# A batched fp32 matmul computed in bf16: manual order, four-byte pair transposes, chunked last loads, and two stores moved behind the last load

## The chip, the cores and the metric

One core of a Trainium2 chip. Times are device microseconds (us), medians of fast runs. Besides its times each kernel has one profiled execution; its *span*, from the first to the last instruction, is 1.7 to 1.9 us shorter than the time of that same execution. In the profiles PE is TensorE, PEld its weight loads, DVE VectorE, ACT ScalarE, POOL GpSimd, SPq the queue that issues the stores.

## The reference

`x` is (32, 512, 1024) fp32, `weight` is (32, 1024, 768) fp32, the output is (32, 512, 768) fp32:

```python
def reference(x, weight):
    return np.matmul(x, weight).astype(np.float32)
```

Each of the 32 batches reads 2.10 MB of x and 3.15 MB of weight and writes 1.57 MB: 218.1 MB altogether. The kernels load with a cast to bf16.

## The kernel before

One batch after another; the Tile scheduler orders the instructions. `x` has its rows on the partitions, so each 128 x 128 block is transposed on TensorE with an identity, copied from PSUM to SBUF, and used as the stationary operand.

```python
w_pool = ...bufs=3; x_pool = ...bufs=3; xT_pool = ...bufs=4; out_pool = ...bufs=3
tpsum = ...bufs=4 (PSUM); mpsum = ...bufs=4 (PSUM)
for b in range(B):
    wb_sb = w_pool.tile([P, KT, N], BF16)
    nc.gpsimd.dma_start(out=wb_sb, in_=w_view[b])
    x_sb = x_pool.tile([P, MT, K], BF16)
    nc.gpsimd.dma_start(out=x_sb, in_=x_view[b])
    out_sb = out_pool.tile([P, MT, N], F32)
    for mt in range(MT):                       # 4 row tiles
        xT_sb = xT_pool.tile([P, KT, P], BF16)
        for j in range(KT):                    # 8 transposes and 8 copies
            pt = tpsum.tile([P, P], BF16)
            nc.tensor.transpose(pt, x_sb[:, mt, j::KT], ident)
            nc.any.tensor_copy(xT_sb[:, j, :], pt)
        for (noff, nsz) in N_SPLITS:           # 512 and 256 columns
            pm = mpsum.tile([P, nsz], F32)
            ...8 matmuls...
            nc.any.tensor_copy(out_sb[:, mt, noff:noff + nsz], pm)
    nc.sync.dma_start(out_view[b], out_sb)
```

Of the kernel before, what the change touches and what calls it, by code (L numbers as in the profile page):

```python
# [1 line left out]

# [5 lines left out]

F32 = mybir.dt.float32
BF16 = mybir.dt.bfloat16  # L10


@with_exitstack
def kernel(
    ctx: ExitStack,
    tc: tile.TileContext,
    x: bass.AP,
    weight: bass.AP,
    out: bass.AP,
):  # L20
    nc = tc.nc
    B, M, K = x.shape
    _, _, N = weight.shape
    P = 128
    assert M % P == 0 and K % P == 0
    MT = M // P
    KT = K // P

    N_SPLITS = []
    off = 0  # L30
    while off < N:
        sz = min(512, N - off)
        N_SPLITS.append((off, sz))
        off += sz

    const = ctx.enter_context(tc.tile_pool(name="const", bufs=1))
    ident = const.tile([P, P], BF16)
    make_identity(nc, ident)

    w_pool = ctx.enter_context(tc.tile_pool(name="w", bufs=3))  # L40
    x_pool = ctx.enter_context(tc.tile_pool(name="x", bufs=3))
    xT_pool = ctx.enter_context(tc.tile_pool(name="xT", bufs=4))
    out_pool = ctx.enter_context(tc.tile_pool(name="out", bufs=3))
    tpsum = ctx.enter_context(tc.tile_pool(name="tpsum", bufs=4, space=bass.MemoryType.PSUM))
    mpsum = ctx.enter_context(tc.tile_pool(name="mpsum", bufs=4, space=bass.MemoryType.PSUM))

    w_view = weight.rearrange("b (ki ko) n -> b ki ko n", ki=P)
    x_view = x.rearrange("b (mi mo) k -> b mi mo k", mi=P)
    out_view = out.rearrange("b (mi mo) n -> b mi mo n", mi=P)

    for b in range(B):
        wb_sb = w_pool.tile([P, KT, N], BF16)
        nc.gpsimd.dma_start(out=wb_sb, in_=w_view[b])  # L53

        x_sb = x_pool.tile([P, MT, K], BF16)
        nc.gpsimd.dma_start(out=x_sb, in_=x_view[b])  # L56

        out_sb = out_pool.tile([P, MT, N], F32)

        for mt in range(MT):  # L60
            xT_sb = xT_pool.tile([P, KT, P], BF16)
            for j in range(KT):
                pt = tpsum.tile([P, P], BF16)
                nc.tensor.transpose(  # L64
                    pt,
                    x_sb[:, mt, j::KT],
                    ident,
                )
                nc.any.tensor_copy(xT_sb[:, j, :], pt)  # L69

            for (noff, nsz) in N_SPLITS:
                pm = mpsum.tile([P, nsz], F32)
                for j in range(KT):
                    nc.tensor.matmul(  # L74
                        pm,
                        xT_sb[:, j, :],
                        wb_sb[:, j, noff:noff + nsz],
                        start=(j == 0),
                        stop=(j == KT - 1),
                    )  # L80
                nc.any.tensor_copy(out_sb[:, mt, noff:noff + nsz], pm)  # L81

        nc.sync.dma_start(out_view[b], out_sb)


# [1 line left out]
_INS = ['x', 'weight']  # L87
_OUTS = [((32, 512, 768), 'float32')]


# [23 lines left out]
```

## Time and profile before

531.46 us (530.21 to 531.87 in three runs), span 528.3 us.

| | before |
|---|---|
| TensorE (PE) busy | 435.0 us, 82% |
| DMA packets, share of 16 engines' span | loads 75.6%, stores 23.0% |
| TensorE idle for weights | 43.8 us |
| first matmul that the last load released, TensorE ends, span ends | 508.7, 521.9, 528.3 us |

The first lines are from the page of the kernel before: DMA busy in tenths over 40 slices, the two big queues, and the two groups of TensorE (busy us, mean ns; then idle time before them and its releaser).

```profile
DMA  8999999999999999999999999999999999999962
q0 software_dynamic: 9216, 83.89, 75.6%
q1 hardware_dynamic: 4608, 50.33, 23.0%
...
L74 PE MATMUL pm<-wb_sb,xT_sb 128*128 128x512 bf16 (+1 forms) x1991 | 382.5, 334 | 47.0 <-DMA wb_sb<-in_weight_dram 43.8
...
L64 PE MATMUL pt<-ident,x_sb 128*128 128x128 bf16 x1024 | 126.7, 226 | 40.0 <-DVE xT_sb L69 22.4
```

DMA is full in every slice but the first and the last two. TensorE is busy 82% and still waits for weights; the other engines idle more. The bound is the transfers. Windows show where they are not full. Columns: start and end, length, busy us of PE, PE weight loads, DVE, ACT and POOL with instruction counts, granted TensorE clock (as a share of full speed), DMA share, and GB/s as written (a load counts with its bf16 bytes, half of what it reads).

```profile
50.00:450.00 400.00, 341.17 (x2376) 225.97 (x2420) 81.38 (x404) 175.09 (x606) 26.37 (x50) 0.97 1.02 265
...
505.00:510.00 5.00, 2.74 (x22) 1.97 (x22) 0.81 (x4) 1.73 (x6) 0.00 (x0) 1.00 0.80 256
510.00:515.00 5.00, 4.82 (x38) 3.34 (x37) 0.81 (x4) 2.31 (x7) 0.00 (x0) 1.00 0.28 118
515.00:520.00 5.00, 4.59 (x36) 3.12 (x36) 1.61 (x8) 2.87 (x11) 0.00 (x0) 1.00 0.01 3
520.00:525.00 5.00, 1.93 (x13) 1.08 (x11) 0.00 (x0) 0.96 (x2) 0.00 (x0) 1.00 0.38 157
```

From 50 to 450 us the DMA share is 1.02 (packets overlap a little, so it can pass 1). After 512 us DMA is nearly idle while TensorE computes the last batch, whose weights have just landed. The timeline shows both ends of that stretch (start us, length, engine, line, instruction; in brackets the idle time before and its releaser):

```profile
508.70 0.38 PE L74 MATMUL pm<-wb_sb,xT_sb 128*128 128x512 bf16 x1 [2.03 <-DMA wb_sb<-in_weight_dram]
...
519.38 2.55 PE L74 MATMUL pm<-wb_sb,xT_sb 128*128 128x512 bf16 x15
...
522.37 0.33 SPq L83 DMA_DIRECT2D out_dram<-out_sb  x1
```

### The profile page before, as it was taken

The numbers are of one execution on the slowest core, as the hardware profiler recorded it, in microseconds if no ns is written. First come the engines' busy times: TensorE is split into PE (matmuls) and PEld (weight loads), VectorE is DVE, ScalarE is ACT, GpSimd is POOL, SyncE is SP. The second block draws the span as 40 slices with busy tenths as digits, with TensorE's granted clock in tenths as the row PEclk, the third lists the DMA queues.
The fourth block names the chain that finished last, engine by engine and source line by source line (L and its number), as shares of the span: only waits on it lengthen the run. The fifth ranks groups of instructions, "written<-read, shape, count | busy, mean of one in ns | idle before, by whom it ended". The sixth has DMA issues, their size and how long they took to land.

```text
span 528.3 us, 7878 instructions
## 1 busy us (share of the span) xinstructions
PE 435.0 (82%) x3015; PEld 287.6 (54%) x3072; DVE 103.4 (20%) x515; ACT 222.8 (42%) x766; POOL 34.6 (7%) x70
## 2 busy tenths in 40 slices
PE   0799979977988897799879889987988897888984
PEld 0466656654656565466545555654555565565653
DVE  0122211211212121122212122221222121221211
ACT  0145534443444344344434444443444344443442
POOL 3000000000000000000000000000000000000000
PEclk9999999998999899899989998998999899998998
DMA  8999999999999999999999999999999999999962
GB/s 163 213 217 276 278 266 268 275 272 257 244 267 273 275 258 269 252 260 275 276 263 244 261 268 273 260 277 257 246 273 275 271 248 265 255 274 275 252 209 120
DMA packets 13861, 134.72 MB, mean 255 GB/s; under 512 B 1536, under 2 KB 1536, under 8 KB 1536
## 3 DMA queue, kind: packets, MB, share of 16 engines
q0 software_dynamic: 9216, 83.89, 75.6%
q1 hardware_dynamic: 4608, 50.33, 23.0%
q8 instruction: 24, 0.39, 0.3%
q14 instruction: 13, 0.11, 0.0%
HBM read 167.77 MB, written 50.33 MB: 413 GB/s over the span
## 4 chain that ended last, share of the span: by engine, by line
issue 81%; DMA 9%; POOL 6%; PE 2%; POOLq 0%; DVE 0%; ACT 0%
DMA wb_sb<-in_weight_dram 6%; POOL wb_sb L53 3%; POOL x_sb L56 3%; DMA x_sb<-in_x_dram 3%; PE pm L74 2%; PE pt L64 0%; DVE xT_sb L69 0%; POOLq L53 0%; POOLq L56 0%; ACT out_sb L81 0%; POOL ident masks.py:199 0%; POOL ident masks.py:197 0%; POOLq masks.py:199 0%; POOLq L109 0%; POOLq L98 0%
## 5 line engine op out<-in xcount | busy, mean ns | idle before, releaser
L74 PE MATMUL pm<-wb_sb,xT_sb 128*128 128x512 bf16 (+1 forms) x1991 | 382.5, 334 | 47.0 <-DMA wb_sb<-in_weight_dram 43.8
L74 PEld LDWEIGHTS <-xT_sb 128*128 128x128 bf16 x2048 | 200.2, 100 | 158.3 <-issue 49.7
L81 ACT COPY out_sb<-pm 128x512 f32<-128x512 f32 (+1 forms) x256 | 122.7, 479 | 207.1 <-PE pm L74 192.6
L69 DVE COPY xT_sb<-pt 128x128 bf16<-128x128 bf16 x515 | 103.4, 222 | 416.3 <-PE pt L64 400.8
L64 PE MATMUL pt<-ident,x_sb 128*128 128x128 bf16 x1024 | 126.7, 226 | 40.0 <-DVE xT_sb L69 22.4
L69 ACT COPY xT_sb<-pt 128x128 bf16<-128x128 bf16 x509 | 111.9, 273 | 91.8 <-PE pt L64 91.3
L64 PEld LDWEIGHTS <-x_sb 128*128 128x128 bf16 x1024 | 102.2, 148 | 75.7 <-issue 48.8
L56 POOL DMA_DIRECT2D x_sb<-in_x_dram x32 | 17.0, 530 | 385.7 <-PE pt L64 385.7
L53 POOL DMA_DIRECT2D wb_sb<-in_weight_dram x32 | 17.1, 533 | 54.2 <-PE pt L64 53.8
L69 ACT ACT_TABLE_LOAD x1 | 1.3, 1283 | 0.7 <-PEq L98 0.7
masks.py:199 POOL TENSOR_SCALAR_AFFINE_SELECT ident<-ident 128x128 bf16<-128x128 bf16 x1 | 0.3, 305 | 0.1
masks.py:197 POOL MEMSET ident<- 128x128 bf16 x1 | 0.2, 205 | 0.3 <-POOLq L98 0.3
L98 POOL MEMSET const-float32-0.0<- 128x1 f32 x1 | 0.1, 98 | 0.2 <-issue 0.2
L98 POOL MEMSET const-bfloat16-1.0<- 128x1 bf16 x1 | 0.1, 101 | 0.0
L98 POOL MEMSET const-uint8-127<- 128x1 uint8 x1 | 0.1, 101 | 0.0
L98 POOL MEMSET const-float32-1.0<- 128x1 f32 x1 | 0.1, 98 | 0.0
## 6 DMA issues: line engine op xcount, KB each, us to landing
wb_sb<-in_weight_dram POOLq DMA_DIRECT2D x32, 1536.0 KB, 34.0
out_dram<-out_sb SPq DMA_DIRECT2D x32, 1536.0 KB, 14.6
x_sb<-in_x_dram POOLq DMA_DIRECT2D x32, 1024.0 KB, 27.0
```

Of the source, the lines that this page charges most:

```text
L53: nc.gpsimd.dma_start(out=wb_sb, in_=w_view[b])
L56: nc.gpsimd.dma_start(out=x_sb, in_=x_view[b])
L64: nc.tensor.transpose(pt, x_sb[:, mt, j::KT], ident,)
L69: nc.any.tensor_copy(xT_sb[:, j, :], pt)
L74: nc.tensor.matmul(pm, xT_sb[:, j, :], wb_sb[:, j, noff:noff + nsz], start=(j == 0), stop=(j == KT - 1),)
L81: nc.any.tensor_copy(out_sb[:, mt, noff:noff + nsz], pm)
L98: nc = _bacc.Bacc("TRN2", target_bir_lowering=False, num_devices=1)
```

## The change

Its intent is to shorten the head and tail and to take work off the engines. x is viewed as fp32 pairs of bf16, so 16 four-byte transposes replace 32 per batch; four share one PSUM bank and one DVE copy. Two row tiles share a tile of three banks, evicted by ACT (1024 columns) and DVE (512). The order is written by hand and loads run four batches ahead. The last two weights come in chunks of (4, 4) and (3, 3, 1, 1) of the 8 rows that a partition holds, with all 16 transposes of such a batch first. The stores of batches 29 and 30 are queued on the load queue behind the last load. Cut to its core:

```diff
+    CHUNKED = {B - 2: (4, 4), B - 1: (3, 3, 1, 1)}
+    HELD = {B - 3, B - 2}
...  # w and x pools 3 -> 5, xT 4 -> 6, out 3 -> 5; tpsum and mpsum 4 -> 2 each
+    def load_w(b):
+        ...
+        for n in CHUNKED.get(b, (KT,)):
+            nc.gpsimd.dma_start(out=ws[b][:, at:at + n, :], in_=w_view[b, :, at:at + n, :])
+    def transpose(b, mt):
+        pt = tpsum.tile([P, JT, P], F32, name="pt")
+        pairs = xs[b].bitcast(F32)
+        for j in range(JT):
+            nc.tensor.transpose(pt[:, j, :], pairs[:, mt, j::JT], ident)
+        xT = xT_pool.tile([P, JT, P, 2], BF16, name="xT")
+        nc.vector.tensor_copy(...)             # 1024 bf16 columns at once
+    def evacuate(b, pair, pm):
+        o = outs[b]
+        nc.scalar.copy(o[:, pair * N2:pair * N2 + 1024], pm[:, 0:1024])
+        nc.vector.tensor_copy(o[:, pair * N2 + 1024:(pair + 1) * N2], pm[:, 1024:N2])
+    with tc.manual_schedule():
+        ...  # x before w; loads of batch b + 4 are issued at batch b
+        for b in range(B):
+            outs[b] = out_pool.tile([P, MT * N], F32, name="out_sb")
+            if b not in CHUNKED:
+                xT = {mt: transpose(b, mt) for mt in (0, 1)}
+                ...  # a pair of row tiles at a time; transposes of tiles 2, 3 in between
+                if b in HELD:
+                    continue
+                nc.sync.dma_start(out_view[b], outs[b])
+            else:
+                xT = {mt: transpose(b, mt) for mt in range(MT)}
+                ...  # chunk by chunk over all four row tiles; the last batch stores by pairs
+            if b == B - 2:
+                for h in sorted(HELD):
+                    nc.gpsimd.dma_start(out=out_view[h], in_=outs[h])
```

More of the change, by code (lines that the diff above doesn't have):

```diff
@@ L24 @@
     P = 128
-    assert M % P == 0 and K % P == 0
     MT = M // P
     KT = K // P
-    N_SPLITS = []
-    off = 0
-    while off < N:
-        sz = min(512, N - off)
-        N_SPLITS.append((off, sz))
-        off += sz
-    const = ctx.enter_context(tc.tile_pool(name="const", bufs=1))
-    ident = const.tile([P, P], BF16)
-    make_identity(nc, ident)
-    w_pool = ctx.enter_context(tc.tile_pool(name="w", bufs=3))
-    x_pool = ctx.enter_context(tc.tile_pool(name="x", bufs=3))
-    xT_pool = ctx.enter_context(tc.tile_pool(name="xT", bufs=4))
@@ L43 @@
-    out_pool = ctx.enter_context(tc.tile_pool(name="out", bufs=3))
-    tpsum = ctx.enter_context(tc.tile_pool(name="tpsum", bufs=4, space=bass.MemoryType.PSUM))
-    mpsum = ctx.enter_context(tc.tile_pool(name="mpsum", bufs=4, space=bass.MemoryType.PSUM))
+    JT = KT // 2
+    N2 = 2 * N
+    CHUNKED = {B - 2: (4, 4), B - 1: (3, 3, 1, 1)}
+    HELD = {B - 3, B - 2}
+    const = ctx.enter_context(tc.tile_pool(name="const", bufs=1))
+    w_pool = ctx.enter_context(tc.tile_pool(name="w", bufs=5))
@@ L47 @@
+    x_pool = ctx.enter_context(tc.tile_pool(name="x", bufs=5))
+    xT_pool = ctx.enter_context(tc.tile_pool(name="xT", bufs=6))
+    out_pool = ctx.enter_context(tc.tile_pool(name="out", bufs=5))
+    tpsum = ctx.enter_context(tc.tile_pool(name="tpsum", bufs=2, space=bass.MemoryType.PSUM))
+    mpsum = ctx.enter_context(tc.tile_pool(name="mpsum", bufs=2, space=bass.MemoryType.PSUM))
     w_view = weight.rearrange("b (ki ko) n -> b ki ko n", ki=P)
     x_view = x.rearrange("b (mi mo) k -> b mi mo k", mi=P)
-    out_view = out.rearrange("b (mi mo) n -> b mi mo n", mi=P)
@@ L51 @@
-    for b in range(B):
-        wb_sb = w_pool.tile([P, KT, N], BF16)
-        nc.gpsimd.dma_start(out=wb_sb, in_=w_view[b])
-        x_sb = x_pool.tile([P, MT, K], BF16)
-        nc.gpsimd.dma_start(out=x_sb, in_=x_view[b])
-        out_sb = out_pool.tile([P, MT, N], F32)
-        for mt in range(MT):
-            xT_sb = xT_pool.tile([P, KT, P], BF16)
-            for j in range(KT):
-                pt = tpsum.tile([P, P], BF16)
-                nc.tensor.transpose(
-                    pt,
-                    x_sb[:, mt, j::KT],
-                    ident,
-                )
-                nc.any.tensor_copy(xT_sb[:, j, :], pt)
-            for (noff, nsz) in N_SPLITS:
-                pm = mpsum.tile([P, nsz], F32)
-                for j in range(KT):
-                    nc.tensor.matmul(
-                        pm,
-                        xT_sb[:, j, :],
-                        wb_sb[:, j, noff:noff + nsz],
-                        start=(j == 0),
-                        stop=(j == KT - 1),
-                    )
-                nc.any.tensor_copy(out_sb[:, mt, noff:noff + nsz], pm)
-        nc.sync.dma_start(out_view[b], out_sb)
+    out_view = out.rearrange("b (mi mo) n -> b mi (mo n)", mi=P)
@@ new lines, with load_x @@
+    xs, ws, outs = {}, {}, {}
+    def load_x(b):
+        xs[b] = x_pool.tile([P, MT, K], BF16, name="x_sb")
+        nc.gpsimd.dma_start(out=xs[b], in_=x_view[b])
+    def load_w(b):
+        ws[b] = w_pool.tile([P, KT, N], BF16, name="w_sb")
+        at = 0
+        for n in CHUNKED.get(b, (KT,)):
+            nc.gpsimd.dma_start(out=ws[b][:, at:at + n, :], in_=w_view[b, :, at:at + n, :])
+            at += n
+    def transpose(b, mt):
[4 more added lines that the diff above has]
+        xT = xT_pool.tile([P, JT, P, 2], BF16, name="xT")
+        nc.vector.tensor_copy(
+            xT.rearrange("p j m r -> p (j m r)"), pt.bitcast(BF16).rearrange("p j m -> p (j m)")
+        )
+        return xT
@@ new lines, with matmuls @@
+    SPLITS = (((0, 512), (512, N - 512)), ((0, 1024 - N), (1024 - N, N2 - 1024)))
+    def matmuls(pm, half, xT, b, kos, together):
+        for ko in kos:
+            for i, (off, size) in enumerate(SPLITS[half]):
+                shares = half == 1 and i == 0
+                nc.tensor.matmul(
+                    pm[:, half * N + off:half * N + off + size],
+                    xT[:, ko // 2, :, ko % 2],
+                    ws[b][:, ko, off:off + size],
+                    start=(ko == 0 and not (together and shares)),
+                    stop=(ko == KT - 1),
+                    skip_group_check=together,
+                )
@@ new lines, in evacuate @@
+    def evacuate(b, pair, pm):
[3 more added lines that the diff above has]
+    with tc.manual_schedule():
+        load_x(0)
+        load_w(0)
+        ident = const.tile([P, P], F32)
+        make_identity(nc, ident)
+        for b in range(1, 4):
+            load_x(b)
+            load_w(b)
+        for b in range(B):
+            if b + 4 < B:
+                load_x(b + 4)
+                load_w(b + 4)
+            outs[b] = out_pool.tile([P, MT * N], F32, name="out_sb")
+            if b not in CHUNKED:
+                xT = {mt: transpose(b, mt) for mt in (0, 1)}
+                for pair in range(2):
+                    pm = mpsum.tile([P, N2], F32, name="pm")
+                    for half in range(2):
+                        if pair == 0:
+                            matmuls(pm, half, xT[half], b, range(KT), False)
+                            xT[2 + half] = transpose(b, 2 + half)
+                        else:
+                            matmuls(pm, half, xT[2 + half], b, range(KT), False)
+                    evacuate(b, pair, pm)
+                if b in HELD:
+                    continue
+                nc.sync.dma_start(out_view[b], outs[b])
+            else:
+                xT = {mt: transpose(b, mt) for mt in range(MT)}
+                pms = [mpsum.tile([P, N2], F32, name="pm") for _ in range(2)]
+                at = 0
+                for n in CHUNKED[b]:
+                    for mt in range(MT):
+                        matmuls(pms[mt // 2], mt % 2, xT[mt], b, range(at, at + n), True)
+                        if at + n == KT and mt % 2 == 1:
+                            evacuate(b, mt // 2, pms[mt // 2])
+                            if b not in HELD:
+                                pair = mt // 2
+                                nc.sync.dma_start(
+                                    out_view[b, :, pair * N2:(pair + 1) * N2],
+                                    outs[b][:, pair * N2:(pair + 1) * N2],
+                                )
+                    at += n
+            if b == B - 2:
+                for h in sorted(HELD):
+                    nc.gpsimd.dma_start(out=out_view[h], in_=outs[h])
```

## The prediction

> **What bounds it now.** The DMA engines, not TensorE. The page's slices show DMA at 90% or more in 38 of 40 slices; its queue table gives loads 75.6% and stores 23.0% of 16 engines' span. PE is 82% busy and waits 43.8 us for weights. In the chain of waits, x loads are issued from 31.5 to 472.2 us in 28 steps, 15.74 us a batch; a batch moves 5.24 MB in (fp32) and 1.57 MB out, so about 430 GB/s. The Trainium skill ("DMA: Bandwidth & Descriptors", section "Where 436 GB/s comes from") gives a ceiling of 435; the trace agrees. All 218.1 MB at 428 to 433 GB/s is 504 to 510 us, starting about 3 us in. The kernel's only sizeable waste is the tail: windows of 5 us show DMA share 0.28, 0.01, 0.38, 0.37 after 510. The last load lands at 508.7, PE works 13.3 us on the last batch (timeline), the last store takes from 522.4 to 528.3. The measured time is 3.1 us above the span.
>
> **What the change does not touch.** Bytes, the fp32-to-bf16 cast in the load, descriptor sizes (8 and 12 KB). Prefetch of five instead of three batches feeds a queue that is never empty. So 15.7 to 15.9 us a batch stays.
>
> **What it removes and adds on the engines.** 1024 bf16 transposes become 512 four-byte ones. Their cost is my main unknown: no trace shows one. The skill ("TensorE: Matmul & The Clock Gate", section "Weight-path perf modes — Fast Weight Load (FWL) and DoubleRow") says fast weight load is off for FP32, so one probably costs more than a bf16 one (four in 0.41 us in the tail); estimate 0.15 to 0.2 us, 0.1 to 0.35 possible. 1024 copies (DVE 222 ns, ACT 273 ns) become 128 on DVE, estimate 1.15 us each (128 columns cost 222 ns). Evictions: 64 on ACT of 1024 columns, estimate 1.0 us (586 and 373 ns for 512 and 256), and 64 on DVE. ACT falls from 223 to about 65 us, DVE rises from 103 to about 190. None is on the critical path while DMA is full. PE needs about 13 to 14 us a batch (16 matmuls take 2.55 us), still under 15.7.
>
> **The tail.** Two stores (3.1 MB, 7.3 us of DMA) move behind the last load, so the last load lands about 4 to 5 us earlier, near 504, and DMA works under the last compute. But without those stores loads come every 12.2 us, below PE's 13 to 14, so the last two or three batches become PE-bound: I expect PE to finish 7 to 12 us after the last load, not at once, which wastes part of the chunking. Then eviction 1 us, issue, and half a store. A hand sum with these durations (it gives 528.8 for before) gives a span of 518 to 525, 520.5 in the middle.
>
> **Prediction:** 523 us, 8 times in 10 within 517.5 to 529.5. Faster by over 2%: 0.31; within 2%: 0.62; slower: 0.07.
>
> **What would show it.** DMA share near 1.02 until about 511, then a gap of some us before the last two half stores; last weight chunk landing near 504; matmuls of the last three batches without waits for weights; PE of the last batch ending 7 to 12 us after the last load.
>
> **What would make it wrong.** Four-byte transposes of 0.1 us or less: PE waits on the last chunk, span about 516, faster by over 2%. At 0.4 us or more PE exceeds 15.7 us a batch and bounds everything: slower. DVE copies holding PE at each batch boundary for over 2 us would act likewise. Weight loads from the interleaved layout slower than 107 ns would slow each 256-column matmul.

## More of the kernel before

The runs of this kernel fall into two groups, near 530.1 and near 531.7; the span, 1.7 to 1.9 us shorter than the time of that same execution, fits the lower one.

I also summed the packet records, counting a load by the fp32 bytes it reads: 427 to 430 GB/s in each 20 us from 60 to 460. The Trainium skill ("DMA: Bandwidth & Descriptors", section "Where 436 GB/s comes from") gives 435.2 GB/s as the ceiling of the 16 SBUF ports, but says that between HBM and SBUF the HBM side, about 358, binds. My figure lies within 2% of the first, but it is counted on the HBM side, where it passes the second; through SBUF went 265 GB/s.

The packet records of the last load end at 508.3 us.

## The result

527.19 us (526.82 to 527.90, four runs) against 531.61 us for the kernel before, beside it on the same chip. The ratio is 0.9934, interval 0.9914 to 0.9955: same, by the 2% rule. Ratios here are the mean time of one kernel's fast runs over that of the other's fast runs of the same rounds, so not quite the ratio of the medians quoted. The span is 525.0 us, 3.3 below before.

The page of the changed kernel (its q0, the load queue, now carries the two held stores too):

```profile
DMA  8999999999999999999999999999999999999982
q0 software_dynamic: 10080, 87.04, 77.6%
q1 hardware_dynamic: 4464, 47.19, 21.7%
...
L78 PE MATMUL pm<-w_sb,xT 128*128 128x256 bf16 (+1 forms) x2048 | 377.0, 344 | 73.8 <-DMA w_sb<-in_weight_dram 63.5
...
L66 DVE COPY xT<-pt 128x1024 bf16<-128x1024 bf16 x128 | 85.1, 686 | 226.8 <-PE pt L64 226.8
L89 ACT COPY out_sb<-pm 128x1024 f32<-128x1024 f32 x64 | 64.7, 1013 | 452.3 <-PE pm L78 452.3
L64 PE MATMUL pt<-ident,x_sb 128*128 128x128 f32 x512 | 79.7, 291 | 12.6 <-DMA x_sb<-in_x_dram 9.7
```

The engines did get lighter: transposes fell from 126.7 to 79.7 us of TensorE time, ACT from 222.8 to 66.0 us in all. But TensorE's busy time in all fell only from 435.0 to 431.3 us: its wait for weights rose from 43.8 to 63.5 us, and from 50 to 450 us its granted clock fell from 0.97 to 0.93. What was saved became waiting and slower matmuls. The windows of the changed kernel, same columns:

```profile
50.00:450.00 400.00, 339.87 (x2013) 219.91 (x2013) 97.32 (x151) 50.65 (x50) 26.37 (x50) 0.93 1.02 265
...
505.00:510.00 5.00, 3.99 (x25) 2.80 (x26) 2.85 (x5) 0.00 (x0) 0.53 (x1) 1.00 0.83 347
510.00:515.00 5.00, 5.00 (x33) 3.04 (x32) 0.00 (x0) 0.00 (x0) 0.00 (x0) 1.00 0.15 61
515.00:520.00 5.00, 2.76 (x17) 1.46 (x15) 1.38 (x2) 1.93 (x2) 0.00 (x0) 1.00 0.06 26
520.00:525.00 5.00, 0.00 (x0) 0.00 (x0) 0.00 (x0) 0.00 (x0) 0.00 (x0) 0.56 0.71 289
```

The steady part is the same to the digit, 1.02 and 265 GB/s. The hole in DMA is still there: the two held stores fill only its beginning (share 0.83), and then DMA waits for TensorE as before. The packet records give the last load's end: 504.4 us, 4 us earlier than before. But TensorE ends at 517.8, 13.4 us after it (before, by the same measure, 13.6). The timeline of the changed kernel shows why:

```profile
476.30 4.37 PE L78 MATMUL pm<-w_sb,xT 128*128 128x512 bf16 x16 [3.79 <-DMA w_sb<-in_weight_dram]
...
489.25 1.11 PE L64 MATMUL pt<-ident,x_sb 128*128 128x128 f32 x8
489.45 1.01 ACT L89 COPY out_sb<-pm 128x1024 f32<-128x1024 f32 x1 [4.66 <-PE pm L78]
490.50 0.69 DVE L90 COPY out_sb<-pm 128x512 f32<-128x512 f32 x1 [4.96 <-ACT out_sb L89]
491.11 1.28 DVE L66 COPY xT<-pt 128x1024 bf16<-128x1024 bf16 x2
...
491.84 1.35 PE L64 MATMUL pt<-ident,x_sb 128*128 128x128 f32 x8 [1.47 <-DVE xT L66]
...
493.02 10.56 PE L78 MATMUL pm<-w_sb,xT 128*128 128x512 bf16 x64
...
507.20 10.56 PE L78 MATMUL pm<-w_sb,xT 128*128 128x512 bf16 x64
517.15 1.93 ACT L89 COPY out_sb<-pm 128x1024 f32<-128x1024 f32 x2 [12.51 <-PE pm L78]
...
518.91 1.25 SPq L131 DMA_DIRECT2D out_dram<-out_sb  x2
519.11 0.69 DVE L90 COPY out_sb<-pm 128x512 f32<-128x512 f32 x1 [0.22 <-ACT out_sb L89]
```

From 476.3 us on TensorE never waits for a load again. Each of the last two batches takes it about 14 us: 3.8 us at the border (503.42 to 507.20) and 10.4 us of matmuls. The last matmuls begin at 507.2, 2.8 us after the last chunk has landed. At the border the copy of the new transposes stands in DVE's order behind an eviction, and that eviction waits for ACT's eviction of *other* columns of the same PSUM tile; the transposes of row tiles 2 and 3 wait 1.47 us for it.

**Theory A.** The steady part is bound by transfers, so only the tail can change. Without the stores of 29 and 30, the last loads come about 12.2 us apart (5.24 MB at 428 GB/s), faster than TensorE's 14; the packet records have them at 492.1 and 504.4. The 4 us that the held stores save turn into a backlog of TensorE. (Only the very last load comes early: the weights of batch 30 end at 492.1 in nohold too, below. What made TensorE late for batch 30 was batch 29, 16.7 us from 476.30 to 493.02, with 16 slow matmuls and a border.) **Rivals.** B: the tail is bound by DMA work, and the held stores or chunks carry what was gained. C: only TensorE's work after the last load counts, wherever stores are held. D: the pair transposes carry the gain.

### The profile page after: what moved, and what is told of

Read it like the earlier page. It is cut to its first block, busy times and chain, and to the rows that moved or that the text cites. A ratio compares the mean times of both kernels' runs of the same rounds, so it can differ in the third digit from the quotient of the medians.

```text
span 525.0 us, 5849 instructions
## 1 busy us (share of the span) xinstructions
PE 431.3 (82%) x2560; PEld 279.3 (53%) x2560; DVE 123.9 (24%) x192; ACT 66.0 (13%) x65; POOL 37.8 (7%) x76
## 4 chain that ended last, share of the span: by engine, by line
PE 80%; another core or an unknown queue 11%; DMA 3%; ACT 2%; issue 2%; DVE 1%; ACTq 0%; POOL 0%; DVEq 0%; POOLq 0%
PE pm L78 70%; PE pt L64 10%; DMA w_sb<-in_weight_dram 3%; ACT out_sb L89 2%; DVE xT L66 1%; DVE out_sb L90 0%; ACTq L164 0%; POOL x_sb L50 0%; DVEq L66 0%; POOLq L153 0%
## 5 line engine op out<-in xcount | busy, mean ns | idle before, releaser
L78 PE MATMUL pm<-w_sb,xT 128*128 128x256 bf16 (+1 forms) x2048 | 377.0, 344 | 73.8 <-DMA w_sb<-in_weight_dram 63.5
L78 PEld LDWEIGHTS <-xT 128*128 128x128 bf16 x2048 | 208.0, 103 | 218.3 <-issue 61.5
L66 DVE COPY xT<-pt 128x1024 bf16<-128x1024 bf16 x128 | 85.1, 686 | 226.8 <-PE pt L64 226.8
L89 ACT COPY out_sb<-pm 128x1024 f32<-128x1024 f32 x64 | 64.7, 1013 | 452.3 <-PE pm L78 452.3
L64 PE MATMUL pt<-ident,x_sb 128*128 128x128 f32 x512 | 79.7, 291 | 12.6 <-DMA x_sb<-in_x_dram 9.7
L64 PEld LDWEIGHTS pt<-ident,x_sb 128*128 128x128 f32 x512 | 76.6, 207 | 19.8 <-issue 11.9
L90 DVE COPY out_sb<-pm 128x512 f32<-128x512 f32 x64 | 43.9, 686 | 169.1 <-ACT out_sb L89 169.1
L56 POOL DMA_DIRECT2D w_sb<-in_weight_dram x36 | 19.1, 531 | 241.2 <-DMA w_sb<-in_weight_dram 212.4
L138 POOL DMA_DIRECT2D out_dram<-out_sb x2 | 1.1, 534 | 28.1 <-DVE out_sb L90 28.1
## 6 DMA issues: line engine op xcount, KB each, us to landing
out_dram<-out_sb POOLq DMA_DIRECT2D x2, 1536.0 KB, 12.3
```

The costliest lines, as they stand in the source:

```text
L56: nc.gpsimd.dma_start(out=ws[b][:, at:at + n, :], in_=w_view[b, :, at:at + n, :])
L64: nc.tensor.transpose(pt[:, j, :], pairs[:, mt, j::JT], ident)
L66: nc.vector.tensor_copy(xT.rearrange("p j m r -> p (j m r)"), pt.bitcast(BF16).rearrange("p j m -> p (j m)"))
L78: nc.tensor.matmul(pm[:, half * N + off:half * N + off + size], xT[:, ko // 2, :, ko % 2], ws[b][:, ko, off:off + size], start=(ko == 0 an ...
L89: nc.scalar.copy(o[:, pair * N2:pair * N2 + 1024], pm[:, 0:1024])
L90: nc.vector.tensor_copy(o[:, pair * N2 + 1024:(pair + 1) * N2], pm[:, 1024:N2])
```

## The experiments

Thirteen further kernels ran. Ratios are against the kernel before of the same call; between calls compare these, since the median of the kernel before moved from 531.6 to 530.2 us with the share of its two groups. By the 2% rule hold3whole and dmaonly are faster, hold2, hold3, hold3split and beforehold2 unclear (their intervals include 0.98), all others the same.

| kernel | median us | ratio | span us |
|---|---|---|---|
| changed kernel | 527.19 | 0.9934 | 525.0 |
| nohold | 526.83 | 0.9936 | 526.8 |
| nochunk | 525.81 | 0.9915 | 523.9 |
| hold2 | 519.79 | 0.9801 | 518.7 |
| hold3 | 518.79 | 0.9783 | 516.9 |
| dmaonly (wrong) | 518.32 | 0.9767 | 516.6 |
| evsplit | 524.19 | 0.9872 | 522.5 |
| bf16t | 525.56 | 0.9912 | 523.6 |
| beforehold | 534.61 | 1.0077 | 533.9 |
| beforehold2 | 519.21 | 0.9789 | 517.3 |
| hold3split | 519.86 | 0.9790 | 518.2 |
| hold3whole | 518.40 | 0.9765 | 516.5 |
| warm29 | 527.03 | 0.9927 | 524.7 |
| warm29b | 526.19 | 0.9910 | 524.7 |

### No stores held: nohold

```diff
-    HELD = {B - 3, B - 2}
+    HELD = set()
```

> The changed kernel with no store held back: all 32 stores go out as soon as their batch is done. Theory A (the tail is bound by TensorE: its last three batches take about 13 to 14 us each and it ends 13 us after the last load): the last weight chunk lands later (508 us in place of 504) but TensorE still ends near 517.5 and the span stays 525.0 within 0.7 us (time 527.2). Theory B (the tail is bound by DMA work and holding two stores saves their 7.3 us partly): span 528 or more.

The time did not move: 526.83 against 527.19, ratios 0.9936 and 0.9934. The last load's packets end at 508.6 in place of 504.4, without any change of the time. (The profiled execution was the longest of its four, 528.74 us with a span of 526.8, outside what I wrote; the median of the times decides. The trace shows why it was long: from 475 to 480 and 480 to 485 us the granted clock was 0.55 and 0.77, in the changed kernel 0.66 and 1.00. So its last batch began 1.4 us later.)

```profile
508.64 10.56 PE L78 MATMUL pm<-w_sb,xT 128*128 128x512 bf16 x62
```

Holding the stores of 29 and 30 bought nothing. B falls for the held stores.

### Last weights whole: nochunk

```diff
-    CHUNKED = {B - 2: (4, 4), B - 1: (3, 3, 1, 1)}
+    CHUNKED = {}
...  # the last batch still stores by pairs, batches 29 and 30 are still held
```

> The changed kernel with the last two weights loaded whole and their batches computed like the others (the last batch still stores by pairs of row tiles, and the stores of batches 29 and 30 are still held). Theory A: the chunks buy nothing since TensorE is behind; batch 30 starts about 1 us later, the first half of the last output is stored 5 us earlier, span 523.5 to 526. Theory B (chunks let TensorE follow the last load closely): a whole weight load delays the last batch's start by 2 to 4 us, span 528 or more.

525.81 us, span 523.9: not slower, if anything 1 us faster. B falls for the chunks too, taken together with their order of work. Chunk order finishes both pairs of row tiles at the end, so both half stores wait for the end; in the ordinary order the first half store was issued at 514.03, 4.9 us before the changed kernel's first.

### Other stores held: hold2 and hold3

```diff
-    HELD = {B - 3, B - 2}
+    HELD = {B - 12, B - 8}               # hold2: batches 20 and 24
+    HELD = {B - 12, B - 8, B - 5}        # hold3: 20, 24 and 27
-    out_pool = ...bufs=5
+    out_pool = ...bufs=3;  held_pool = ...bufs=len(HELD)
```

> The changed kernel, but the two stores held for the end are those of batches 20 and 24 in a pool of their own (out pool 3 deep in place of 5), not 29 and 30. Same bytes, same engine work. Theory A says that holding the stores of the last batches speeds up the loads of just those batches beyond TensorE's pace and so builds a backlog; held from earlier batches, the same time is gained where TensorE has slack: w29 lands near 468 in place of 476, TensorE ends near 508 to 510 and the span is 516 to 519. Theory C (what limits the end is only the TensorE work after the last load, wherever stores are held): span 524 to 526.

> As hold2 with three held: batches 20, 24 and 27. Theory A: TensorE ends near 506 to 508, DMA has 11 us of stores left for it to hide behind, and the span is the DMA floor, 514.5 to 517, DMA busy to the end. Theory C: 524 to 526.

hold2: 519.79 us, hold3: 518.79 us. The bytes and the engine work are those of the changed kernel; only *which* store waits differs (in hold3 also how many), and 7.4 and 8.4 us of the medians are gone, 7 and 8 by the ratios. Theory C would have them unchanged. The windows of hold3, and its last matmuls:

```profile
500.00:505.00 5.00, 5.00 (x33) 3.04 (x31) 0.00 (x0) 0.00 (x0) 0.00 (x0) 1.00 1.01 424
505.00:510.00 5.00, 3.09 (x19) 1.66 (x17) 1.20 (x2) 1.93 (x2) 0.00 (x0) 1.00 0.83 351
510.00:515.00 5.00, 0.00 (x0) 0.00 (x0) 0.18 (x1) 0.00 (x0) 0.00 (x0) 0.61 0.83 345
...
497.58 10.56 PE L79 MATMUL pm<-w_sb,xT 128*128 128x512 bf16 x62
```

The hole is nearly closed (share 0.83 or more in each 5 us up to 515): DMA works through TensorE's last batch. The last load's packets end at 497.2 and TensorE ends near 508.1 (62 recorded matmuls from 497.58, 10.56 us), 9.6 us earlier than in the changed kernel. A store held back from batch 20 moves all later loads forward while TensorE still has slack (14 of 15.9 us a batch); one held back from batch 29 moves only a load that TensorE can't use yet. By the packet records the weights of batch 29 end at 475.8 us in the changed kernel, 468.7 in hold2 and 464.5 in hold3. The clock is no rival here: hold2 had a longer slow stretch at batch 29 than the changed kernel (0.75 and 0.57 from 465 to 470 and 470 to 475 us) and was still 6.3 us of span shorter; hold3 had none.

### Transfers alone: dmaonly

```diff
-    ...transposes, matmuls, evictions...
+    # a few columns of each load are copied, so that buffers come free as loads land
+    nc.sync.dma_start(out_view[b], outs[b])      # of a tile filled with zeros
```

> No TensorE work at all; wrong result on purpose. The same loads (same chunks, same order, 5 buffers) and 32 whole stores, each sent when its batch's weights have landed. It measures the time that the transfers alone need. Theory A (transfers set 15.7 us a batch, the rest is tail): span 515 to 518, from 218.1 MB at 428 GB/s, 3.5 us of start and the last store behind the last load. Rival (transfers are held up by buffers and compute even in the steady part): 512 or less.

518.32 us, span 516.6, and in its window from 50 to 450 us (no TensorE columns here) the same share and rate as the real kernels:

```profile
50.00:450.00 400.00, 32.38 (x100) 37.33 (x26) 29.38 (x50) 1.00 1.02 264
```

So the rival, that buffers or compute hold up the steady part, falls. The kernel before was 11.7 us of span above this run, the changed one 8.4, hold3 0.3. It is no strict floor: its own last store waits for the last load.

### The PSUM tile split: evsplit

```diff
-    pm = mpsum.tile([P, N2], F32)
+    pm = mpsum.tile([P, 1024], F32), mpsum.tile([P, 512], F32)
```

> The changed kernel, with the three-bank PSUM tile as two tiles (1024 and 512 columns), so that the DVE eviction no longer waits for the ACT eviction of the other columns. Theory A: at each of the last two batch borders the copies of the transposes start 1.0 to 1.7 us earlier, TensorE's wait of 1.5 us there falls to about 0.5, and the last DVE eviction ends 0.7 to 1 us earlier: span 521.5 to 523.5 (time 523.7 to 525.7), the steady part unchanged at 15.9 us a batch. Rival (these waits are hidden): 524.5 to 526.

524.19 us, span 522.5, as expected. DVE no longer waits for ACT, and the wait of the transposes at the border falls from 1.47 to 0.43 us:

```profile
491.20 1.35 PE L64 MATMUL pt<-ident,x_sb 128*128 128x128 f32 x8 [0.43 <-DVE xT L66]
...
515.30 1.93 ACT L93 COPY out_sb<-pm 128x1024 f32<-128x1024 f32 x2 [11.51 <-PE pm L78]
515.52 1.29 DVE L94 COPY out_sb<-pm 128x512 f32<-128x512 f32 x2 [9.12 <-PE pm L78]
```

The last eviction, now ACT's, ends at 517.2 in place of 519.8. About 2.5 us of the changed kernel's tail were this one dependency, paid at two borders and at the end.

### bf16 transposes: bf16t

```diff
-    pt = tpsum.tile([P, JT, P], F32);  4 transposes of xs[b].bitcast(F32)[:, mt, j::JT]
+    pt = tpsum.tile([P, KT, P], BF16); 8 transposes of xs[b][:, mt, j::KT]
```

> The changed kernel with bf16 transposes (32 a batch, eight to a PSUM bank, one 1024-column copy as before) in place of 16 four-byte ones. Theory A: only the TensorE time of the last three batches counts; a four-byte transpose took 0.12 to 0.14 us there, a bf16 one should take 0.06 to 0.1, so 16 x 0.14 = 2.2 us a batch against 2 to 3: span 524.5 to 527.5. Rival (pair transposes carry the gain): 529 or more.

525.56 us, span 523.6: not slower than with pairs, so rival D falls (and the span is 0.9 us under what I wrote). In the tail 16 bf16 transposes take as long as 8 four-byte ones:

```profile
488.02 1.16 PE L63 MATMUL pt<-ident,x_sb 128*128 128x128 bf16 x16
```

against 1.11 us for x8 at 489.25 above. That is 0.07 us apiece against 0.14. What pairs do halve is the instruction count; the batching of copies is kept in this run, and is not tested here. Its last borders fall 1.3 us earlier because here batch 29 waited only 1.65 us for its weights and ran its first 16 matmuls in 2.76 us, not 4.37:

```profile
476.64 2.76 PE L77 MATMUL pm<-w_sb,xT 128*128 128x512 bf16 x15 [1.65 <-DMA w_sb<-in_weight_dram]
```

Apart from this slow stretch, worth 1.3 us, the two are level (spans 523.6 and 525.0).

### The kernel before, with three stores held: beforehold, beforehold2

```diff
+    # in short, not word for word
+    HELD = {B - 12: None, B - 8: None, B - 5: None}      # tiles of a pool of their own
+    if b == B - 1:        # a tie to the last load of x, so that the scheduler can't hoist the stores
+        zero = x_sb[:, 0, 0:8] * 0.0
+        for h in sorted(HELD):
+            HELD[h][:, 0, 0:8] += zero
+            nc.gpsimd.dma_start(out=out_view[h], in_=HELD[h])
```

> The kernel before, its scheduler, three buffers and bf16 transposes left alone, with only the stores of batches 20, 24 and 27 held (own pool) and queued behind the last load. Theory A says that this part alone has the gain: the last load lands near 497.5, TensorE ends 13.5 us later near 511, the last store runs from 512 to 518: span 516.5 to 519.5, time 519.5 to 522.5, 2% faster than before. Rival (the gain of hold3 needs the manual order, the deep prefetch or the pair transposes): span 524 or more.

beforehold took 534.61 us, span 533.9. By the number that is the rival's range, but the run settles nothing, by a fault of mine: the tie ran on DVE, in front of the copies that TensorE needs, and TensorE stood for 16.7 us.

```profile
486.65 0.17 DVE L66 TENSOR_SCALAR zero<-x_sb 128x8 f32<-128x8 bf16 x1 [18.40 <-DMA x_sb<-in_x_dram]
...
487.37 0.27 PE L76 MATMUL pt<-ident,x_sb 128*128 128x128 bf16 x1 [16.68 <-DVE xT_sb L81]
```

beforehold2 has the same tie on GpSimd, which is idle then.

> beforehold again, with the tie that keeps the held stores late on GpSimd and not on VectorE, where it blocked the copies for 18.4 us and TensorE for 16.7 us. Theory A as before: last load near 497.5, TensorE ends near 511, span 516.5 to 519.5. Rival (the gain needs the rest of the change): 524 or more.

519.21 us, span 517.3: 2.1% below before, interval 1.8 to 2.4%. With its scheduler, three buffers, 32 transposes and 32 small copies a batch all left alone, the kernel before gets within 0.5 us of hold3 from the placing of three stores (and three more output buffers for them). The gain of hold3 needs nothing else of the change.

### Beyond hold3: hold3split and hold3whole

hold3split joins hold3 and evsplit; hold3whole is hold3 with the last two weights loaded whole.

> hold3 and evsplit together. Theory A: TensorE ends near 505 in place of 507.5, the last half stores join the held ones before DMA runs dry, span 514.5 to 516 (time 516.3 to 518). If the transfer floor (dmaonly 516.6) can't be passed: same as hold3, 516.5 to 517.5.

> hold3 with the last two weights loaded whole and computed like the others (last batch stored by pairs). Theory A: in hold3 TensorE needed the last weights at 497.5 and they had landed at 497.2, so chunks buy nothing there: span 515.5 to 517.5. Rival (chunks matter once DMA holds the tail): 518.5 or more.

hold3split missed: 519.86 us, 1 us slower than hold3 by the medians (0.4 us by the ratios), although TensorE ended almost 4 us earlier (504.3). Now the transfers bind the end, and an earlier TensorE has nothing to give: the last packets end at 515.7 us, in hold3 at 515.5. Its span is 1.3 us longer because 2.4 us pass from the last packet to the end, in hold3 1.3; why is open. hold3whole, 518.40 us, confirms that chunks buy nothing there either; it is the fastest correct kernel, 2.35% under before, but not apart from hold3.

### The clock at batch 29: warm29, warm29b

```diff
+    if b == B - 3:      # after its first transposes, before its first matmul
+        spare = tpsum.tile([P, 512], F32, name="pt")
+        for _ in range(16):                 # warm29b: 9
+            nc.tensor.matmul(spare, ws[b - 1][:, 1, 0:P], ws[b - 1][:, 0, 0:512], start=True, stop=True)
```

> The changed kernel, with 16 matmuls whose result nobody reads (3.4 us) while TensorE waits for the weights of batch 29. In the changed kernel the wait was 3.8 us, the granted clock then 0.5, and the next 16 matmuls took 4.37 us in place of 2.76. Theory A: as TensorE is never free again before the end, those 1.6 us are on the path: span 523 to 524. If the slow matmuls are hidden: 524.7 to 525.5.[...]

> warm29 with 9 idle matmuls in place of 16. In warm29 they kept the clock up (the 16 matmuls after them took 2.76 us, not 4.37) but began only after a DVE copy (474.1) and ended at 477.4, 0.8 us after the weights had landed, which gave back most of it. Nine should end near 476.1, before the landing. Theory A: the first 16 matmuls of batch 29 take 2.8 us from 476.5, TensorE ends near 516 and the span is 523.2 to 524 (time 525.2 to 526.2). If nothing is gained: 524.7 to 525.3.

In both, the first 16 matmuls took 2.76 us, so keeping TensorE busy did keep the clock here:

```profile
477.59 2.76 PE L78 MATMUL pm<-w_sb,xT 128*128 128x512 bf16 x16
```

But both spans are 524.7, the edge of what I had written for "nothing gained" (times 527.03 and 526.19 us; the second lies in A's range of times, but the two were not run in one call with the changed kernel). The idle matmuls waited for a PSUM buffer (behind DVE) and held TensorE until the batch's own first matmul at 477.59 and 477.61 us (in warm29b since batch 28 itself ended later), in the changed kernel 476.30. So 1.3 of the 1.6 us gained were given back. The slow clock is a term of at most 1.6 us; how much of it can be had back stays open.

## Why the prediction was right or wrong

- **"What bounds it now. The DMA engines."** Right: share 1.02 and 265 GB/s from 50 to 450 us before and after, and dmaonly has the same.
- **"So 15.7 to 15.9 us a batch stays."** Right.
- **"The last load lands ... near 504."** Right: 504.4.
- **"The last two or three batches become PE-bound."** Right, and the mechanism behind the small gain: nohold, hold2 and hold3 show it. But of the loads only the last came 12.3 us after the one before; batch 29 still waited 3.79 us, and batch 30 was late through batch 29.
- **"I expect PE to finish 7 to 12 us after the last load ... Then eviction 1 us."** This is the step that failed, in size: what TensorE still has to do after the last load, and the eviction after it. It was 13.4 us, then 2.0 us from the last matmul (517.8) to the end of the last eviction (519.8). I forecast a gain of 8.5 us and 4.4 came. The 41.5 us from the first matmul of batch 29 (476.3) to TensorE's end are 31.3 us of matmuls at full clock, 1.6 more because 16 of them were slow, 1.0 of transposes inside batch 29 and two borders of 3.8. The terms I had not counted: (1) in each border 2.2 us are transposes at 0.14 us (my estimate, 0.15 to 0.2, was a little high) and 1.5 are waiting for DVE behind ACT, which I had not seen in the code (my list of what would make it wrong names over 2 us of this); (2) the last eviction was serial for the same reason; evsplit took most of both away and gained 2.5 us of span; (3) the first 16 matmuls of batch 29 ran 1.6 us slow after a 3.8 us wait. Without the two waits and the slow clock, by this sum, TensorE would have ended 8 to 9 us after the last load, inside my range. The middle of my span, 520.5, plus 2.5 and 1.6 is 524.6; measured was 525.0. This sum is arithmetic: the first part is shown by evsplit, the 1.6 us only by the trace (the warm runs got back 0.3).
- **"Then ... half a store."** Wrong: with chunk order both halves come at the end (two issues from 518.91); nochunk, which stores the first pair earlier, has 1.1 us less span.
- **DVE copies "estimate 1.15 us each".** Wrong, 0.69 us; at the two borders they do stand on TensorE's path, but cheaper than I had put them.
- **"The measured time is 3.1 us above the span."** Wrong: I set the median beside the span of an execution of the faster group. It is 1.7 to 1.9 us in every execution where both are known. So the middle of my span, 520.5, stands for a time of 522.3, not 523: this error of mine hid 0.7 us of the other, by luck.

The time lay in the range and the class (same) was the likeliest, but the range was wide (12 us). What carries the 3.3 us of span that the change did gain is not shown: without the held stores, the chunks or the four-byte transposes it is still there, and no run takes apart the manual order, the batched copies, x before w and the deeper pools. The traces only say where it lies: in nohold, with the last load at 508.6 as before (508.3), TensorE ended 10.6 us after it and not 13.6, with the transposes of the last batch done by then. What I missed as a designer is that the remedy was in my own diagnosis: I wrote that holding the last stores makes the last batches PE-bound, and did not ask which stores could be held without that.

## What to carry to other kernels

Where, as here, transfers bind the steady part, what is gained in the tail is what keeps the transfer queue filled while the last batch computes. Hold back work that is already done early, from a stage where the other engine has slack, and not from the last stage, where the transfers so freed only run into that engine's own pace. Before splitting loads finer, check in the timeline that the engine really waits for the last piece.

## What the Trainium skill lacked or had wrong

- "TensorE: Matmul & The Clock Gate" gives in "Part 4: PE-mode transpose" durations for a bf16 transpose only (~390 ns alone, ~275 ns in a kernel). In a row, bf16 ones came every 0.07 us here (16 in 1.16 us) and four-byte ones every 0.14 us (8 in 1.11 us), with recorded lengths of 228 and 291 ns.
- The same page, "Weight-path perf modes — Fast Weight Load (FWL) and DoubleRow", says that FP32 has no fast weight load, but gives no duration for an fp32 one. The trace agrees in direction: 207 ns for a recorded fp32 weight load of a transpose, 148 ns for a bf16 one of the same tile.
- On the clock the page lacked nothing that these runs show. Its "Part 1: The HAM clock gate (the "warmup" mystery)" gives an idle window of about 3.4 us before the clock halves, and its Part 4 says that a transpose does not count as busy in the same way. The trace agrees: counted from the start of the transposes to the next matmul that is none, gaps of 4.92 us (changed kernel, 3.79 of it waiting) and 3.31 us (evsplit, 2.19 waiting) were followed by slow matmuls (16 in 4.37 us, 15 recorded in 4.44 us), one of 2.81 us (bf16t, 1.65 waiting) was not (2.76 us). No run isolates the transposes.
- "DMA: Bandwidth & Descriptors" names engines 7 and 15 as usually slower, but not that the end of a queue drains unevenly. When the loads of the kernel before ran out, only 9 to 11 packets were in flight from 505 to 507 us, against a median of 16 from 50 to 450; in hold3 8 or 9 from 508.75 to 510. The trace does not say which engines.
